# Where a decoder layer's matmul operands begin in SBUF, and a shorter product of P and V

## The chip, the core and the metric

The kernel runs on one core of a Trainium2 chip. Its time is the time of one execution on the device in microseconds (us), as the median of several runs. One further execution is recorded by the hardware profiler; all rows called profile come from it. A core has a matrix engine (TensorE, PE in the profile; PEld is its loading of the stationary operand, the "weights" of a matmul), VectorE (DVE), ScalarE (ACT), GpSimd (POOL) and SyncE (SP, which here issues the transfers). They work on two memories on the chip: SBUF, with 128 partitions, in which all tiles below lie, and PSUM, into which matmuls write. A tile begins at the same byte in each partition it uses, and "remainder" below is that byte modulo 512.

## The reference

One layer of a decoder with 256 positions and 2048 channels, in float32. Cut to what matters:

```python
h = rmsnorm(x, pre_mix_g)
proj = h @ w_in                  # q, k, v of two groups of heads, and forget gates
o_a = swa_sink_attention(...)    # 16 heads, 2 key/value heads, window 128, sinks, ALiBi
o_b = forgetting_attention(...)  # 16 heads, decay from the forget gates
mix = concatenate([rmsnorm(o_a), rmsnorm(o_b)]) @ w_out
x = x + rmsnorm(mix, post_mix_g)
h = rmsnorm(x, pre_ffn_g)
u = causal_dwconv(h @ w_up)      # width 3; 2 x 5632 channels
gate, val = split(u, 2)
x = x + rmsnorm((gelu(gate) * val) @ w_down, post_ffn_g)
```

## The kernel before

**High and low parts.** To keep float32 accuracy with TensorE's fp32r type, each operand a is kept as two tiles: a high part, a rounded to fp32r, and a low part, the rest. A product is three matmuls: high by high, low by high, high by low. The weights come from memory in units of up to 1024 columns (`w_load`, tile `raw`); ACT writes the high part (L104, tile `whi`) and DVE the low part (L107, tile `wlo`), each in one of five rotating buffers. The activations lie as high part in columns 0 to 255 and low part in columns 256 to 511 of one row: `hT` (16 blocks of 128 channels, the normed and transposed input), `oT` (16 tiles, attention's output) and `G` (22 tiles, the gated channels).

**Which operand is held.** A matmul has a held operand of 128 columns, loaded ahead of it, and a moving one that streams past it. In the projections to q and k and to the feed-forward channels (`proj_T`, `unit_T`) the weights are held and hT moves. A high pass (L247) streams 512 columns, both parts of hT, past a block of `whi`; a low pass (L254) streams the 256 high columns past a block of `wlo`. For each pair of output blocks the runs are: 16 matmuls of the high pass for blocks 0 to 7 of hT, 32 of the low pass for all blocks, 16 of the high pass for blocks 8 to 15. In `mm3` (L269) the roles are exchanged: a block of hT (V projection), oT (output projection) or G (down projection) is held, and 512 columns of `whi` or `wlo` move. There, six matmuls in a row belong to one tile: for each half of the positions high by `whi`, high by `wlo`, low by `whi`.

**Where the tiles begin.** Rows of hT, oT and G have 520 elements, of which 512 are used (`WIDE = 520`, 2080 bytes). So block k of hT begins at remainder 32k, and each tile of oT and G begins 32 bytes further on than the one before it in SBUF. `raw`, `whi` and `wlo` have 1024 columns and begin at multiples of 512, except for eight tiles of a later pool that hold parts of the output projection.

**Attention.** Work for a pair of heads is cut into stages (`tables`, `scores`, `transposes`, `pv`), which `later` and `tick` put between the units of the projections, so that TensorE has projections to do while DVE and ACT work on the softmax. In `pv` both parts of V are held: 128 columns for a pair of heads, the same 64 values twice in the first group, where two heads share them. P's parts `ph` and `pl` stream past them, 512 columns (L478) and then 256 (L480). The upper 64 rows of the result are one head's output and the lower 64 the other's, each in its own columns. ACT and DVE take these from PSUM (L487 to L489).

**Order.** TensorE's instructions stand in the order in which the program is written (`manual_schedule`). The other engines are ordered by a scheduler outside a few written stretches.

Of the kernel before, what the change touches and what calls it, by code (L numbers as in the profile page):

```python
# [17 lines left out]
P = 128  # L18
# [4 lines left out]
KT = D // P  # L23
EPS = 1e-6
NEG = -1e30
FHALF = 22
HOLD = 6
WIDE = 520


@with_exitstack
def hybrid_layer(ctx: ExitStack, tc: tile.TileContext, x, pre_mix_g, w_in, b_forget, sinks,
# [3 lines left out]
    pe, act, dve, pool, sp = nc.tensor, nc.scalar, nc.vector, nc.gpsimd, nc.sync  # L36
# [4 lines left out]
    const = ctx.enter_context(tc.tile_pool(name="const", bufs=1))  # L41
    main = ctx.enter_context(tc.tile_pool(name="main", bufs=1))
    wp = ctx.enter_context(tc.tile_pool(name="wp", bufs=4))
    small = ctx.enter_context(tc.tile_pool(name="small", bufs=4))
    ps = ctx.enter_context(tc.tile_pool(name="ps", bufs=1, space=PSUM))

    ctx.enter_context(tc.manual_schedule(engines={mybir.EngineType.PE}))

    def bank(tag="acc"):
# [14 lines left out]
    UNIT = 1024  # L64
    WB = 5

    def w_load(src, a, c, pin=False):
        raw = wp.tile([P, UNIT], F32, tag="raw", bufs=5, name="raw")
        i = sp.dma_start(raw[:, :a * c].rearrange("p (a c) -> p a c", a=a), src)
        if pin:  # L70
            tc.keep_in_program_order(i)
        return raw, a, c

    def w_parts(n, keep=None):

        if keep and keep[0] is None:
            return keep[1]
        where, pre, nb = (keep[0], "h", keep[1]) if keep else (wp, "w", WB)
        return [where.tile([P, UNIT], F32R, tag=pre + x, bufs=nb, name="w" + x)[:, :n]
                for x in ("hi", "lo")]  # L80

    def w_high(unit, keep=None):

        raw, a, c = unit
        n = a * c
        hi, lo = w_parts(n, keep)
        act.copy(hi, raw[:, :n])

        def low():
            dve.tensor_tensor(lo, raw[:, :n], hi.bitcast(F32), op=ALU.subtract)  # L90

        return [x.rearrange("p (a c) -> p a c", a=a) for x in (hi, lo)], low

    def w_split(unit, pin=False, keep=None, begun=None, between=None):

        raw, a, c = unit
        n = a * c
        hi, lo = begun or w_parts(n, keep)
        for i in range(2 if between else 1):
            cs = slice(i * 512, i * 512 + 512) if between else slice(0, n)  # L100
            if i:
                between()
            if not between or i:
                i1 = act.copy(hi[:, cs], raw[:, cs])  # L104
                if pin:
                    tc.keep_in_program_order(i1)
            i2 = dve.tensor_tensor(lo[:, cs], raw[:, cs], hi[:, cs].bitcast(F32), op=ALU.subtract)  # L107
            if pin:
                tc.keep_in_program_order(i2)
        return [x.rearrange("p (a c) -> p a c", a=a) for x in (hi, lo)]  # L110

    def w_unit(src, a, c, keep=None):
        return w_split(w_load(src, a, c), keep=keep)

    def w_rows(w, k0, a, c0, c):
        return w[k0 * P:(k0 + a) * P, c0:c0 + c].rearrange("(a p) c -> p a c", p=P)
# [10 lines left out]
    gpre = const.tile([16, P], F32, tag="gpre", name="gpre")  # L127
# [7 lines left out]
    for i in range(2):  # L135
        cs = slice(i * 256, (i + 1) * 256)
# [26 lines left out]
    gcol = const.tile([P, 48], F32, tag="gcol", name="gcol")  # L163
# [9 lines left out]
        pool.tensor_tensor(r, v, mhalf, op=ALU.pow)  # L173
        return r

    hT = main.tile([P, KT, WIDE], F32R, tag="hT", name="hT")
    def to_T(srcs, t0, n, g0, pin=False):

        for part in range(2):
# [91 lines left out]
    def split(hi, lo, src):  # L271
        act.copy(hi, src)
        dve.tensor_tensor(lo, src, hi.bitcast(F32), op=ALU.subtract)

    with tc.tile_pool(name="mixp", bufs=1) as mp:
        oT = [mp.tile([P, WIDE], F32R, tag="oT", bufs=16, name=f"oT{j}")[:, 0:512] for j in range(16)]
        sqs = mp.tile([P, 2, S], F32, tag="sqs", name="sqs")

        att = tc.tile_pool(name="att", bufs=1)
        ap = att.__enter__()  # L280
# [44 lines left out]
        begun = w_parts(UNIT)  # L325
# [4 lines left out]
        for u in range(4):  # L330
            if u:
                parts = w_split(first[0][u], True)
            else:
                parts = w_split(first[0][u], True, begun=begun,
                                between=lambda: x_part(0, (1,), "acc"))
# [17 lines left out]
            unit_T(parts, u, bq0)  # L353


        gst = const.tile([32, P], F32, tag="gst", name="gst")
        sp.dma_start(gst[0:16, :], pre_ffn_g.rearrange("o (a p) -> (o a) p", p=P))
        sp.dma_start(gst[16:24, :], grp_swa_g.rearrange("o (a p) -> (o a) p", p=P))
        sp.dma_start(gst[24:32, :], grp_fox_g.rearrange("o (a p) -> (o a) p", p=P))
# [24 lines left out]
            pool.affine_select(out=u, in_=u, compare_op=ALU.is_ge, fill=0.0, base=base,  # L384
                               pattern=[[1, 256]], channel_multiplier=-1)

        vpa = ap.tile([P, 2, 2, 2, P], F32R, tag="vpa", name="vpa")
        vpb = main.tile([P, 2, 2, 8, P], F32R, tag="x", name="vpb")

        NK = 3  # L390
# [27 lines left out]
        def attend(j, q, ki, values, table, h0, sink, at):  # L418
# [53 lines left out]
            def pv():  # L472
                ph, pl = st["h"], st["l"]
                o = bank("att")
                ov = o.rearrange("p (e q) -> p e q", e=2)
                passes = ((0, ph), (1, ph), (0, pl))
                for n, (hl, p) in enumerate(passes):
                    pe.matmul(ov, values(hl, 0), p[:, :, 0:256], start=(n == 0), stop=False)  # L478
                for n, (hl, p) in enumerate(passes):
                    pe.matmul(ov[:, :, P:256], values(hl, 1), p[:, :, 256:384], start=False,  # L480
                              stop=(n == 2))
                sq = ap.tile([P, 256], F32, tag="sqo", bufs=1, name="sqo")
                for e in range(2):
                    r = slice(e * 64, (e + 1) * 64)
                    g = gcol[r, 32 + j:33 + j]
                    hi, lo = oT[j][r, 0:256], oT[j][r, 256:512]
                    act.activation(hi, ov[r, e, :], AF.Copy, scale=g)  # L487
                    act.activation(sq[r, :], ov[r, e, :], AF.Square)
                    dve.scalar_tensor_tensor(lo, ov[r, e, :], g, hi.bitcast(F32), op0=ALU.mult,  # L489
                                             op1=ALU.subtract)  # L490
# [13 lines left out]
        def swa_pair(p, q, at):  # L504
            def table(t):
                for e in range(2):
                    slope = 2.0 ** (-8.0 * (2 * p + e + 1) / H)
                    pool.tensor_scalar(t[:, e, 0:256], dist, -slope, None, op0=ALU.mult)
                    pool.tensor_scalar(t[:, e, 256:384], dist[:, P:256], -slope, None,
                                       op0=ALU.mult)  # L510

            attend(p, q, p // 4, lambda hl, t: vpa[:, hl, t, p // 4, :], table, 2 * p, True, at)

        cq = ap.tile([P, 2, H], F32, tag="cq", name="cq")

# [23 lines left out]
        def kv_a():  # L539
            k32 = scratch()  # L540
            evac_sum(bkv[0], k32, rowk)
            ksw = scratch()
            sp.dma_start(ksw[64:128, :], k32[0:64, :])
            sp.dma_start(ksw[0:64, :], k32[64:128, :])
            for i, (e_src, o_src) in enumerate(((k32, ksw), (ksw, k32))):
                for r, src in zip(halves, (e_src, o_src)):
                    split(khi[i][r, :], klo[i][r, :], src[r, :])
            v32 = scratch()
            evac_sum(bkv[1], v32, rowk)

            def v_T():
                vb = bank("att")
                for t in range(2):
                    pe.transpose(vb[:, t * P:(t + 1) * P], v32[:, t * P:(t + 1) * P], ident)
                vv = vb[:, :256].rearrange("p (t k d) -> p t k d", t=2, k=2)
                for e in range(2):
                    split(vpa[:, 0, :, :, e * 64:(e + 1) * 64],
                          vpa[:, 1, :, :, e * 64:(e + 1) * 64], vv)

            later(3, v_T)  # L560

# [121 lines left out]
        out_half(1, evac_b, range(2))  # L683


        hT2 = main.tile([P, KT, WIDE], F32R, tag="hT", name="hT2")
        hT = hT2
        dffn, rmix = [], []
        sq2 = [small.tile([P, 4], F32, tag=f"sqm{t}", bufs=1, name=f"sqm{t}") for t in range(2)]
# [53 lines left out]
        for n in (2, 3):  # L743
            for u in range(4):
                raw = w_load(w_rows(w_out, 8 + u * 2, 2, n * 512, 512), 2, 512)
                (hi, lo), low = w_high(raw, (hp, 4) if n == 2 else None)
# [41 lines left out]
    with tc.tile_pool(name="ffn", bufs=1) as fp:  # L788
# [87 lines left out]
        ysq = [small.tile([P, 5], F32, tag=f"ysq{t}", bufs=1, name=f"ysq{t}") for t in range(2)]  # L876
        gbf = None
        for half in range(2):
            G = [fp.tile([P, WIDE], F32R, tag="G", bufs=FHALF, name=f"G{j}")[:, 0:512]
                 for j in range(FHALF)]  # L880
            for g in range(FHALF // 2):
                c0 = (half * (FHALF // 2) + g) * 256
# [75 lines left out]
        held = []  # L958
# [61 lines left out]
```

## Time and profile before

| | |
|---|---|
| runs | 1096.8, 1095.73, 1096.19 us; median 1096.19 |
| profiled execution | 1095.65 us, its span 1093.9 us |
| TensorE, matmul | 1082.4 us busy (99%), 6002 instructions |
| TensorE, loading of weights | 930.1 us busy (85%) |
| VectorE, ScalarE | 729.3 us (67%), 613.7 us (56%) |
| mean traffic | 185 GB/s; HBM read 199.58 MB |
| granted TensorE clock | 0.998 of full speed |

The span runs from the first to the last instruction; the execution's time holds 1.75 us more. A row of a group gives line, engine, operation and tiles (written <- read), then busy time and the mean duration of one in ns, then the idle time before it. A matmul's duration is longer than the step from its start to the next one's start, since each begins while the one before it drains. So steps are read from starts, or from a run of known length.

### The profile page before, as it was taken

How to read it: one execution, taken by the hardware profiler on the slowest of the kernel's cores; microseconds unless marked ns; L12 is line 12 of the kernel's file. 1: busy time of each engine (PE TensorE's matmuls, PEld its weight loads, DVE VectorE, ACT ScalarE, POOL GpSimd, SP SyncE). 2: the span in 40 equal slices, each digit the busy share in tenths (PEclk: the TensorE clock that was granted, in tenths of full speed). 3: DMA queues.
4: the chain of work that ended last, by engine and by line, in shares of the span. 5: the costliest groups of instructions: out<-in, count | busy, mean ns of one | idle time of the engine just before them, and what ended most of it. 6: DMA issues, size and time to landing. Idle time of an engine off the chain costs nothing.

```text
span 1093.9 us, 16309 instructions
## 1 busy us (share of the span) xinstructions
PE 1082.4 (99%) x6002; PEld 930.1 (85%) x6002; DVE 729.3 (67%) x1193; ACT 613.7 (56%) x1069; POOL 223.5 (20%) x252
## 2 busy tenths in 40 slices
PE   9999999999999999999999999999999999999996
PEld 7899988888889888888888888888888888888886
DVE  5977767776468876777677444457777777755453
ACT  7766766667547655556555443446555555644450
POOL 3342343441022212112121000002121211201111
PEclk9999999999999999999999999999999999999999
DMA  8645557554863766666655665666566656656552
GB/s 290 207 117 168 173 155 220 164 161 151 288 218 117 228 187 184 191 192 191 187 183 182 198 189 188 188 188 192 177 192 189 185 184 192 190 193 187 185 169 78
DMA packets 164971, 202.88 MB, mean 185 GB/s; under 512 B 6780, under 2 KB 130972, under 8 KB 164380
## 3 DMA queue, kind: packets, MB, share of 16 engines
q1 hardware_dynamic: 164176, 201.27, 59.3%
q8 instruction: 47, 0.77, 0.3%
q10 hardware_dynamic: 716, 0.58, 0.2%
q14 instruction: 32, 0.26, 0.1%
HBM read 199.58 MB, written 2.11 MB: 184 GB/s over the span
## 4 chain that ended last, share of the span: by engine, by line
PE 97%; DVE 1%; ACT 1%; DMA 0%; issue 0%; POOL 0%; SPq 0%; DVEq 0%; POOLq 0%; ACTq 0%
PE bank_acc L269 35%; PE bank_acc L247 22%; PE bank_att L247 14%; PE bank_acc L254 12%; PE bank_att L254 7%; PE bank_att L434 1%; PE bank_att L478 1%; PE bank_att L469 1%; PE bank_att L211 1%; PE bank_acc L211 1%; PE bank_att L480 1%; DVE wlo L107 0%; DMA x_in<-in_x_dram 0%; PE bank_att L216 0%; DVE hT L715 0%; PE bank_acc L216 0%
## 5 line engine op out<-in xcount | busy, mean ns | idle before, releaser
L107 DVE TENSOR_TENSOR wlo<-raw,whi 128x1024 fp32r<-128x1024 f32 (+3 forms) x357 | 429.4, 1211 | 265.4 <-ACT whi L104 256.0
L104 ACT CAST whi<-raw 128x1024 fp32r<-128x1024 f32 (+3 forms) x356 | 363.0, 1033 | 291.4 <-issue 140.9
L247 PE MATMUL bank_acc<-hT,whi 128*128 128x512 f32 x1088 | 263.9, 395 | 0.0
L247 PEld LDWEIGHTS bank_acc<-hT,whi 128*128 128x128 f32 x1088 | 200.6, 188 | 43.7
L269 PE MATMUL bank_acc<-whi,G 128*128 128x512 f32 (+1 forms) x724 | 217.8, 383 | 0.0
L824 POOL TENSOR_TENSOR u<-u,rowf 128x256 f32<-128x256 f32 x88 | 96.8, 1121 | 508.2 <-DVE u L823 505.9
L269 PEld LDWEIGHTS bank_acc<-whi,G 128*128 128x128 f32 x724 | 133.6, 188 | 29.4
L247 PE MATMUL bank_att<-hT,whi 128*128 128x512 f32 x640 | 153.6, 394 | 0.0
L247 PEld LDWEIGHTS bank_att<-hT,whi 128*128 128x128 f32 x640 | 118.8, 188 | 26.8
L254 PE MATMUL bank_acc<-hT,wlo 128*128 128x256 f32 x1088 | 139.5, 282 | 0.0
L254 PEld LDWEIGHTS bank_acc<-hT,wlo 128*128 128x128 f32 x1088 | 135.3, 188 | 4.4
L269 PE MATMUL bank_acc<-wlo,G 128*128 128x512 f32 (+1 forms) x362 | 138.9, 384 | 0.0
L269 PE MATMUL bank_acc<-whi,oT 128*128 128x512 f32 (+1 forms) x272 | 83.5, 383 | 0.0
L269 PEld LDWEIGHTS bank_acc<-wlo,G 128*128 128x128 f32 x362 | 68.0, 188 | 14.6
L254 PEld LDWEIGHTS bank_att<-hT,wlo 128*128 128x128 f32 x640 | 78.5, 188 | 1.8
L254 PE MATMUL bank_att<-hT,wlo 128*128 128x256 f32 x640 | 79.1, 281 | 0.0
L269 PEld LDWEIGHTS bank_acc<-whi,oT 128*128 128x128 f32 x272 | 50.1, 188 | 10.3
L269 PE MATMUL bank_acc<-wlo,oT 128*128 128x512 f32 (+1 forms) x136 | 51.8, 381 | 0.0
L269 PE MATMUL bank_acc<-whi,hT 128*128 128x384 f32 (+1 forms) x192 | 47.7, 325 | 0.0
L826 ACT ACTIVATE yg<-u,cw 128x256 f32<-128x256 f32 x44 | 26.5, 602 | 26.7 <-POOL u L824 26.7
L826 ACT ACTIVATE yv<-u,cw 128x256 f32<-128x256 f32 x44 | 26.5, 602 | 25.9 <-POOL u L824 25.9
L452 ACT ACTIVATE p<-p,nm 128x256 f32<-128x256 f32 (+1 forms) x64 | 28.4, 445 | 20.3 <-DVE nm L440 20.3
(195 smaller groups left out, 1012.5 us busy)
## 6 DMA issues: line engine op xcount, KB each, us to landing
raw<-in_w_up_dram SPq DMA_DIRECT2D x176, 512.0 KB, 3.6
raw<-in_w_down_dram SPq DMA_DIRECT2D x88, 512.0 KB, 4.6
raw<-in_w_in_dram SPq DMA_DIRECT2D x51, 512.0 KB, 4.3
raw<-in_w_out_dram SPq DMA_DIRECT2D x32, 512.0 KB, 4.4
raw<-in_w_in_dram SPq DMA_DIRECT2D x16, 384.0 KB, 3.7
cb<-c_dram SPq DMA_DIRECT2D x8, 256.0 KB, 3.4
x_sb<-in_x_dram SPq DMA_DIRECT2D x2, 1024.0 KB
raw<-in_w_in_dram SPq DMA_DIRECT2D x5, 408.0 KB, 3.5
```

The source lines that it names most:

```text
L104: i1 = act.copy(hi[:, cs], raw[:, cs])
L107: i2 = dve.tensor_tensor(lo[:, cs], raw[:, cs], hi[:, cs].bitcast(F32), op=ALU.subtract)
L211: pe.matmul(b, hi[:, a, m * P:(m + 1) * P], hT[:, kt, 0:512], start=(kt == 0), stop=(kt == KT - 1))
L247: pe.matmul(b, hi[:, a, m * P:(m + 1) * P], hT[:, kt, 0:512], start=(kt == 0), stop=(last == (0, kt)))
L254: pe.matmul(b[:, 256:512], lo[:, a, m * P:(m + 1) * P], hT[:, u * 4 + a, 0:256], start=False, stop=(last == (1, u * 4 + a)))
L269: pe.matmul(b, a, r[:, cols], start=(first and i == 0), stop=(last and i == 2))
L434: pe.matmul(sb[e][:, cs], a[r, t * P:(t + 1) * P], b[r, 0:nk], start=(n == 0), stop=(n == 2))
L452: act.activation(p[:, e, cs], p[:, e, cs], AF.Exp, bias=nm[:, t, e:e + 1], scale=-1.0, accum_out=rs[:, t, e:e + 1])
L469: pe.transpose(pb[:, i * P:(i + 1) * P], p[:, e, c:c + P], ident)
L478: pe.matmul(ov, values(hl, 0), p[:, :, 0:256], start=(n == 0), stop=False)
L824: pool.tensor_tensor(u[:, 2:258], u[:, 2:258], rowf, op=ALU.mult)
L826: act.activation(y, u[:, 2:258], AF.Identity, bias=cw[:, 3, ch:ch + 1], scale=cw[:, 2, ch:ch + 1])
```

## The change

**Where operands begin.** The rows of hT, oT and G have 512 elements now. A filler before hT puts all its 16 blocks at remainder 192 (a filler behind it, one in the small pool and the reuse of `gpre`'s tile for `gst` bring what comes after to where it is wanted). All tiles of oT and G, and all tiles of moving weights, begin at multiples of 512. High parts that are held still begin there too. Low parts get buffers of 1152 columns in the common pool: as moving operand they begin at the buffer's start, as held operand 56 elements (224 bytes) behind it (`LOW`, argument `held`).

**The first group's V.** Its tile held 64 high values twice, and 64 low values twice in another block. Now one block holds the 64 high values beside the 64 low ones (`vpa`, half as large), and `pv` makes two passes, `ph` and `pl`, instead of three. The result's upper 64 rows are P by high and its lower 64 rows P by low, for both heads; so ACT copies the lower rows to a tile `half`, DVE adds them to the upper rows into a scratch tile, and the gain, the square and the low part of oT are then made from that for both heads at once. P low by V low is added by this as well, which was left out before.

```diff
+LOW = 56
+ROOM = 112
+    small.tile([P, ROOM], F32, tag="room", bufs=1, name="room")
...
+    def w_parts(n, keep=None, held=True):
...
+        hi = where.tile([P, UNIT], F32R, tag=pre + "hi", bufs=nb, name="whi")
+        if where is not wp:
+            lo = where.tile([P, UNIT], F32R, tag=pre + "lo", bufs=nb, name="wlo")
+            return hi[:, :n], lo[:, :n]
+        lo = where.tile([P, UNIT + 128], F32R, tag=pre + "lo", bufs=nb, name="wlo")
+        return hi[:, :n], lo[:, LOW * held:LOW * held + n]
...
     def w_unit(src, a, c, keep=None):
-        return w_split(w_load(src, a, c), keep=keep)
+        return w_split(w_load(src, a, c), keep=keep, held=False)
...
-    hT = main.tile([P, KT, WIDE], F32R, tag="hT", name="hT")
+    main.tile([P, 48], F32, tag="before_hT", name="before_hT")
+    hT = main.tile([P, KT, 512], F32R, tag="hT", name="hT")
+    main.tile([P, 80], F32, tag="behind_hT", name="behind_hT")
...
-        oT = [mp.tile([P, WIDE], F32R, tag="oT", bufs=16, name=f"oT{j}")[:, 0:512] for j in range(16)]
+        oT = [mp.tile([P, 512], F32R, tag="oT", bufs=16, name=f"oT{j}")[:, 0:512] for j in range(16)]
...
-        gst = const.tile([32, P], F32, tag="gst", name="gst")
+        gst = const.tile([32, P], F32, tag="gpre", name="gst")
...
-        vpa = ap.tile([P, 2, 2, 2, P], F32R, tag="vpa", name="vpa")
+        vpa = ap.tile([P, 2, 2, P], F32R, tag="vpa", name="vpa")
...
-                passes = ((0, ph), (1, ph), (0, pl))
+                passes = ((0, ph), (0, pl)) if sink else ((0, ph), (1, ph), (0, pl))
...
+                if sink:
+                    half = ap.tile([64, 512], F32, tag="half", bufs=1, name="half")
+                    act.copy(half, o[64:128, :])
+                    ob = scratch()
+                    for e in range(2):
+                        cs = slice(e * 256, (e + 1) * 256)
+                        dve.tensor_tensor(ob[e * 64:(e + 1) * 64, :], o[0:64, cs], half[:, cs],
+                                          op=ALU.add)
+                    g = gcol[:, 32 + j:33 + j]
+                    hi, lo = oT[j][:, 0:256], oT[j][:, 256:512]
+                    act.activation(hi, ob, AF.Copy, scale=g)
+                    act.activation(sq, ob, AF.Square)
+                    dve.scalar_tensor_tensor(lo, ob, g, hi.bitcast(F32), op0=ALU.mult,
+                                             op1=ALU.subtract)
...
-                for e in range(2):
-                    split(vpa[:, 0, :, :, e * 64:(e + 1) * 64],
-                          vpa[:, 1, :, :, e * 64:(e + 1) * 64], vv)
+                split(vpa[:, :, :, 0:64], vpa[:, :, :, 64:128], vv)
...
-            G = [fp.tile([P, WIDE], F32R, tag="G", bufs=FHALF, name=f"G{j}")[:, 0:512]
+            G = [fp.tile([P, 512], F32R, tag="G", bufs=FHALF, name=f"G{j}")[:, 0:512]
```

Where operands begin changes no order. P times V does. On TensorE, around the first `pv` of the first group (between low passes of a projection; `vpa` is V, `ph` and `pl` are P's parts), before:

```order
L254 MATMUL bank_acc<-hT,wlo 128x256 x8
L478 MATMUL bank_att<-ph,vpa 128x512 x2
L478 MATMUL bank_att<-pl,vpa 128x512
L480 MATMUL bank_att<-ph,vpa 128x2x128 x2
L480 MATMUL bank_att<-pl,vpa 128x2x128
L254 MATMUL bank_acc<-hT,wlo 128x256 x8
```

And of the change (L487 and L489 are the lines before's L478 and L480, L263 is L254):

```order
L263 MATMUL bank_acc<-hT,wlo 128x256 x8
L487 MATMUL bank_att<-ph,vpa 128x512
L487 MATMUL bank_att<-pl,vpa 128x512
L489 MATMUL bank_att<-ph,vpa 128x2x128
L489 MATMUL bank_att<-pl,vpa 128x2x128
L263 MATMUL bank_acc<-hT,wlo 128x256 x8
```

One matmul of each width has gone, and the place between the low passes is the same. On ACT, which takes the result from PSUM, at the first pair, before:

```order
L452 ACTIVATE p,rs<-p,nm 128x128 x2
L487 ACTIVATE oT_114<-bank_att,gcol 64x256
L488 ACTIVATE sqo<-bank_att 64x256
L449 ACTIVATE es<-es 128x4
L399 COPY scr<-bank_acc 128x256 x2
L487 ACTIVATE oT_114<-bank_att,gcol 64x256
L488 ACTIVATE sqo<-bank_att 64x256
```

And of the change:

```order
L461 ACTIVATE p,rs<-p,nm 128x128 x2
L494 COPY half<-bank_att 64x512
L408 COPY scr<-bank_acc 128x256
L458 ACTIVATE es<-es 128x4
L408 COPY scr<-bank_acc 128x256
L111 CAST whi<-raw 128x768
L502 ACTIVATE oT_117<-scr,gcol 128x256
L503 ACTIVATE sqo<-scr 128x256
```

The four operations of 64 rows have become one copy of 64 rows and two operations of 128 rows; these two stand behind the copy and DVE's two additions.

More of the change, by code (lines that the diff above doesn't have):

```diff
@@ L27 @@
 HOLD = 6
-WIDE = 520
+LOW = 56
+ROOM = 112
 @with_exitstack
@@ L72, in w_load @@
         return raw, a, c
-    def w_parts(n, keep=None):
+    def w_parts(n, keep=None, held=True):
         if keep and keep[0] is None:
@@ L78, in w_parts, with w_high @@
         where, pre, nb = (keep[0], "h", keep[1]) if keep else (wp, "w", WB)
-        return [where.tile([P, UNIT], F32R, tag=pre + x, bufs=nb, name="w" + x)[:, :n]
-                for x in ("hi", "lo")]
-    def w_high(unit, keep=None):
+        hi = where.tile([P, UNIT], F32R, tag=pre + "hi", bufs=nb, name="whi")
[4 more added lines that the diff above has]
+        return hi[:, :n], lo[:, LOW * held:LOW * held + n]
+    def w_high(unit, keep=None, held=True):
         raw, a, c = unit
         n = a * c
-        hi, lo = w_parts(n, keep)
+        hi, lo = w_parts(n, keep, held)
         act.copy(hi, raw[:, :n])
@@ L92, in w_high, with w_split @@
         return [x.rearrange("p (a c) -> p a c", a=a) for x in (hi, lo)], low
-    def w_split(unit, pin=False, keep=None, begun=None, between=None):
+    def w_split(unit, pin=False, keep=None, begun=None, between=None,
+                held=True):
         raw, a, c = unit
         n = a * c
-        hi, lo = begun or w_parts(n, keep)
+        hi, lo = begun or w_parts(n, keep, held)
         for i in range(2 if between else 1):
@@ L480, in pv @@
                     pe.matmul(ov[:, :, P:256], values(hl, 1), p[:, :, 256:384], start=False,
-                              stop=(n == 2))
+                              stop=(n == len(passes) - 1))
                 sq = ap.tile([P, 256], F32, tag="sqo", bufs=1, name="sqo")
-                for e in range(2):
+                if sink:
[12 more added lines that the diff above has]
+                                             op1=ALU.subtract)
+                for e in () if sink else range(2):
                     r = slice(e * 64, (e + 1) * 64)
@@ L510, in table @@
                                        op0=ALU.mult)
-            attend(p, q, p // 4, lambda hl, t: vpa[:, hl, t, p // 4, :], table, 2 * p, True, at)
+            attend(p, q, p // 4, lambda hl, t: vpa[:, t, p // 4, :], table, 2 * p, True, at)
         cq = ap.tile([P, 2, H], F32, tag="cq", name="cq")
@@ L555, in v_T @@
                 vv = vb[:, :256].rearrange("p (t k d) -> p t k d", t=2, k=2)
-                for e in range(2):
-                    split(vpa[:, 0, :, :, e * 64:(e + 1) * 64],
-                          vpa[:, 1, :, :, e * 64:(e + 1) * 64], vv)
+                split(vpa[:, :, :, 0:64], vpa[:, :, :, 64:128], vv)
             later(3, v_T)
@@ L683, in hybrid_layer @@
         out_half(1, evac_b, range(2))
-        hT2 = main.tile([P, KT, WIDE], F32R, tag="hT", name="hT2")
+        hT2 = main.tile([P, KT, 512], F32R, tag="hT", name="hT2")
         hT = hT2
@@ L745, in hybrid_layer @@
                 raw = w_load(w_rows(w_out, 8 + u * 2, 2, n * 512, 512), 2, 512)
-                (hi, lo), low = w_high(raw, (hp, 4) if n == 2 else None)
+                (hi, lo), low = w_high(raw, (hp, 4) if n == 2 else None, False)
                 low()
```

## The prediction

> **What bounds the kernel now.** I read the page first, then the chain in order of time, then rows of TensorE (PE) in ever smaller windows.
>
> ```profile
> PE 1082.4 (99%) x6002; PEld 930.1 (85%) x6002; DVE 729.3 (67%) x1193; ACT 613.7 (56%) x1069; POOL 223.5 (20%) x252
> ...
> PE 97%; DVE 1%; ACT 1%; DMA 0%; issue 0%; POOL 0%; SPq 0%; DVEq 0%; POOLq 0%; ACTq 0%
> ```
>
> PE works 99% of the span and is 97% of the chain. Of all its waits for others the longest is at the start:
>
> ```profile
> PE bank_acc L159 <- DVE junk L154: 1.3, 1, 1.3
> ```
>
> So time can be won only inside the matmul stream: fewer matmuls, or less time from one start to the next. The chain in order of time gives that step for long runs:
>
> ```profile
> 375.41 7.43 PE bank_att L247 x32
> ...
> 592.44 122.82 PE bank_acc L269 x528
> ```
>
> A 512-wide matmul takes 7.43/32 = 232.2 ns in the high passes of `proj_T` (L247, hT moves) and 122.82/528 = 232.6 ns in the down projection (L269, weights move, G is loaded). These are means. The ninth group of six in that block belongs to G8, since 592.44 + 8 x 6 x 0.2326 = 603.6; here are PE's rows from G7 into G8, and the L269 rows of the two windows (durations as minimum/median/maximum, ns):
>
> ```profile
> 602.28 0.40 PE L269 MATMUL bank_acc<-wlo,G 128*128 128x512 f32 x1
> 602.51 0.63 PE L269 MATMUL bank_acc<-whi,G 128*128 128x512 f32 x2
> 602.98 0.40 PE L269 MATMUL bank_acc<-wlo,G 128*128 128x512 f32 x1
> ...
> 603.68 0.39 PE L269 MATMUL bank_acc<-wlo,G 128*128 128x512 f32 x1
> 603.90 0.62 PE L269 MATMUL bank_acc<-whi,G 128*128 128x512 f32 x2
> 604.36 0.39 PE L269 MATMUL bank_acc<-wlo,G 128*128 128x512 f32 x1
> ```
>
> ```profile
> L269 PE MATMUL bank_acc<-wlo,G x2: 395/396/396, 602.3 to 603.0; 128*128 128x512 f32 x2
> ...
> L269 PE MATMUL bank_acc<-wlo,G x2: 389/389/389, 603.7 to 604.4; 128*128 128x512 f32 x2
> ```
>
> Three matmuls take 0.70 us (233 ns each) before G8 and 0.68 us (227 ns) at G8. The shown duration follows: 396 there, 389 here, so step = duration - 162, which I use below. Nothing differs but addresses. In this kernel a G tile is 2080 bytes, so each begins 32 bytes later than its neighbour modulo 512; in the built program G8 (byte 188416) begins at a multiple of 512, as do the moving weights. The weight load of the next matmul reads while this one streams, and how the two addresses stand to each other is worth 6 ns.
>
> The hT rows do the same with the roles exchanged. The kernel sweeps all sixteen remainders and gets their mean; the change fixes one. In one feed-forward stretch:
>
> ```profile
> 382.68 3.96 PE L254 MATMUL bank_att<-hT,wlo 128*128 128x256 f32 x32
> 386.48 3.88 PE L247 MATMUL bank_att<-hT,whi 128*128 128x512 f32 x16
> 390.19 3.89 PE L247 MATMUL bank_acc<-hT,whi 128*128 128x512 f32 x16
> 393.92 3.94 PE L254 MATMUL bank_acc<-hT,wlo 128*128 128x256 f32 x32
> ```
>
> A low pass (L254, 256 wide) takes (386.48 - 382.68)/32 = 118.8 ns a matmul.
>
> **The change part by part.** First the matmuls whose loaded operand is G or oT (L269), 512 wide:
>
> ```profile
> L269 PE MATMUL bank_acc<-whi,G 128*128 128x512 f32 x652 | 206.2, 394 | 0.0
> ...
> L269 PE MATMUL bank_acc<-wlo,G 128*128 128x512 f32 x326 | 128.8, 395 | 0.0
> L269 PE MATMUL bank_acc<-whi,oT 128*128 128x512 f32 x240 | 77.3, 396 | 0.0
> L269 PE MATMUL bank_acc<-wlo,oT 128*128 128x512 f32 x120 | 47.3, 395 | 0.0
> ```
>
> That is 1338. After the change each stands as G8 does now: both operands at multiples of 512. At best all go from 232.6 to 226.7: -7.9 us. The group's mean is a little over that, since the stream reaches the quick step only after its first matmuls; I take 227.6: 1338 x 5.0 ns = **-6.7 us**. At worst oT, broken up by attention, gains nothing and G settles half way: -2.5 us.
>
> Second, the high passes: all of hT at remainder 192, weights at 0. Today only block 6 of hT (6 x 32) stands so. Its two matmuls come in two sorts. One window of each sort, each with the last matmul of block 5 (397 in both), then all of L247 and L254:
>
> ```profile
> L247 PE MATMUL bank_att<-hT,whi x3: 388/392/397, 381.5 to 382.0; 128*128 128x512 f32 x3
> ...
> L247 PE MATMUL bank_acc<-hT,whi x3: 394/397/399, 392.8 to 393.2; 128*128 128x512 f32 x3
> ...
> L247 PE MATMUL bank_acc<-hT,whi x1088: 388/394/504, 32.5 to 961.8; 128*128 128x512 f32 x182
> L247 PE MATMUL bank_att<-hT,whi x640: 388/394/399, 367.7 to 939.4; 128*128 128x512 f32 x160
> ...
> L254 PE MATMUL bank_acc<-hT,wlo x1088: 276/281/387, 36.3 to 958.2; 128*128 128x256 f32 x182
> L254 PE MATMUL bank_att<-hT,wlo x640: 276/281/287, 371.5 to 935.8; 128*128 128x256 f32 x160
> ```
>
> The first pair is 392 and 388 (230 and 226 ns), the second 399 and 394 (237 and 232). The first ends on the quickest step of all (388), the second falls from its first to its second matmul. At G8 the quick step, once reached, held over the three steps shown; so I lean to the quick pair and take 230 ns against 232.2: 1728 x 2.2 = **-3.8 us**. Bounds: 388 throughout is -10.0 us; the second pair's mean of 234.5 is +4.0 us.
>
> Third, the low passes, 1728 of 256 columns: hT at 192, loaded low parts at 224. No row today has a loaded operand off a multiple of 512 in such a pass. By difference, 192 - 224 is -32, as block 15 has today (480 against 0). It too comes in two sorts; each window holds blocks 14 and 15:
>
> ```profile
> L254 PE MATMUL bank_att<-hT,wlo x4: 283/284/287, 386.0 to 386.4; 128*128 128x256 f32 x4
> ...
> L254 PE MATMUL bank_acc<-hT,wlo x4: 279/282/282, 397.2 to 397.6; 128*128 128x256 f32 x4
> ```
>
> They lie on both sides of the median, 281, so I take **0**. Bounds: 276 throughout (-5 ns) is -8.6 us. For the dear end I use block 6, at 192 against 0 today:
>
> ```profile
> L254 PE MATMUL bank_att<-hT,wlo x5: 280/282/287, 383.9 to 384.3; 128*128 128x256 f32 x5
> ```
>
> Its two are 282 and 287, mean 284.5, +3.5 ns: +6.0 us.
>
> Fourth, the first group's P times V: four matmuls in place of six, for eight pairs of heads.
>
> ```profile
> 58.19 0.63 PE L478 MATMUL bank_att<-ph,vpa 128*128 128x512 f32 x2
> 58.66 0.39 PE L478 MATMUL bank_att<-pl,vpa 128*128 128x512 f32 x1
> 58.88 0.40 PE L480 MATMUL bank_att<-ph,vpa 128*128 128x256 f32 x2
> 59.13 0.28 PE L480 MATMUL bank_att<-pl,vpa 128*128 128x256 f32 x1
> ```
>
> One 512-wide goes, (58.66 - 58.19)/2 = 0.235 us, and one 256-wide, (59.13 - 58.88)/2 = 0.125 us: 8 x 0.36 = **-2.9 us**. PE doesn't wait for what follows. Per pair ACT now does:
>
> ```profile
> L487 ACT ACTIVATE oT<-bank_att,gcol 64x256 fp32r<-64x256 f32 x14 | 6.5, 464 | 2.9 <-DVE oT L489 2.9
> L488 ACT ACTIVATE sqo<-bank_att 64x256 f32<-64x256 f32 x14 | 5.1, 365 | 0.0
> L591 ACT ACTIVATE vpb<-bank_acc,rpre 128x384 fp32r<-128x384 f32 x4 | 2.1, 575 | 0.6 <-PE bank_acc L269 0.6
> ...
> L489 DVE SCALAR_TENSOR_TENSOR oT<-bank_att,gcol,oT 64x256 fp32r<-64x256 f32 x14 | 6.7, 481 | 2.4 <-ACT sqo L488 2.2
> ```
>
> That is 2 x (464 + 365) = 1.66 us on ACT and 2 x 0.48 on DVE. After: one copy of 512 columns (about 0.6, an estimate from L591's 575 ns for 384), one activation, one square, 1.4 us; DVE three operations of about 0.48, +0.5 us, or 4 us over the eight pairs. DVE is 67% busy over the span, so this is hidden; with that cover gone it is those 4 us. The new wait is DVE's for the copy `half`, and queued behind it are splits of weights (L107) that PE needs only units later. The DMA of `gst` now shares the first gains' tile, whose one reader runs in the first 5 us. No price.
>
> Fifth, the V projection also loads hT at 192 now, some 300 matmuls: within +-6 ns each, +-1.8 us; I take 0.
>
> Sum: -6.7 - 3.8 + 0 - 2.9 = -13.4 us on the profiled execution's 1095.65 (span 1093.9 and 1.75 around it) gives 1082.2. The median of the runs lies 0.5 above that execution, so **1082.7**, say 1083.
>
> Against all this speaks a rule of the Trainium skill, "SBUF — State Buffer", section "Who interferes with whom": TensorE has separate ports for moving operand and weight load, and never waits on anyone. By it only the fourth part would count. The trace differs: 396 against 389 ns at G7 and G8.
>
> **The rivals.** *Both passes lock*: high at 388, low at 276, L269 at 226.7: -10.0 - 8.6 - 7.9 - 2.9 = -29.4, 1067. For it: the quick step held at G8 once reached, and a constant remainder gives it time. Against it: block 6's second sort, and its low matmuls of 282 and 287.
>
> *Addresses do nothing*, and the quick rows have another reason, such as their place in the unit: then only P times V counts, 1096.2 - 2.9 = 1093.3. For it speaks only the rule just named. Against it: the G7 and G8 rows, in the same places of their groups.
>
> *One remainder settles slow*: sixteen remainders average out, one need not. If the high passes sit at 234.5 (+4.0), the low ones at block 6's mean (+6.0) and L269 gains only its worst bound of 2.5, then 4.0 + 6.0 - 2.5 - 2.9 = +4.6, 1100.8. It decides from where the two passes lose over 5.4 us together. For it: the second sort; against: the pairs fall from 237 to 232, so that sort doesn't look lasting.
>
> **How the numbers follow.** Forecast, 1074 to 1091: 60%. Both lock, below that: 17%. Nearly only P times V, 1091 to 1096: 13%. Settles slow: 10%. The range 1069 to 1094 leaves out about 5% below and 14% above. About 0.2% (2.2 us) is what a measurement of this kernel can tell from no change. Faster by more, below 1094: 0.60 + 0.17 + 0.09 = 0.86. Within it: 0.06; slower: 0.08.
>
> **What would show it.** In the changed profile: L269's 512-wide rows at a mean near 390 in place of 394 to 396, and a down projection of 528 matmuls in about 120.2 us in place of 122.8. The high rows near 392; the low rows near 281; in the row of P times V 8 matmuls of `ph,vpa` of each width in place of 16; idle time of PE unchanged. I am wrong if L269's mean stays at 394, if the low rows move more than 2 ns either way, or if PE begins to wait for `whi`, `wlo` or `oT`.

## The result: 1086.9 us after 1096.1, and the profile after

| | before | after |
|---|---|---|
| runs | 1095.73 to 1096.8, median 1096.07 | 1086.57 to 1087.42, median 1086.9 |
| profiled execution, its span | 1095.65, 1093.9 us | 1086.65, 1084.9 us |

The ratio is 0.9916, with a 95% interval of 0.9899 to 0.9933: 9.2 us less, where 13.4 were forecast. The first part of the page of the kernel after, and the shares of its chain:

```profile
PE 1073.4 (99%) x5986; PEld 926.5 (85%) x5986; DVE 734.1 (68%) x1200; ACT 613.6 (57%) x1060; POOL 224.8 (21%) x252
...
PE 96%; DVE 1%; ACT 1%; DMA 1%; SPq 0%; issue 0%; POOL 0%; DVEq 0%; POOLq 0%; ACTq 0%
```

TensorE (PE) is still the whole of it. Outside its busy time the span holds 1084.9 - 1073.4 = 11.5 us, and before it held 1093.9 - 1082.4 = 11.5. So in sum no waiting came or went; all 9.0 us lie inside the matmul stream. The chain in order of time says in which stage. Its rows give start, length (us) and what ran. First before, then after, where `mm3` is now L278, the high pass L256 and the low pass L263:

```profile
282.92 50.31 PE bank_acc L269 x216
...
371.63 3.78 PE bank_att L254 x32
...
592.44 122.82 PE bank_acc L269 x528
...
722.77 7.44 PE bank_acc L247 x32
...
962.24 123.08 PE bank_acc L269 x594
```

```profile
279.82 49.13 PE bank_acc L278 x216
...
367.34 3.78 PE bank_att L263 x32
371.12 7.46 PE bank_att L256 x32
...
588.28 119.70 PE bank_acc L278 x528
...
715.50 7.47 PE bank_acc L256 x32
...
955.70 120.64 PE bank_acc L278 x594
```

The stages between these rows, in us:

| stage | before | after | difference |
|---|---|---|---|
| start to the long block of the output projection | 282.92 | 279.82 | -3.10 |
| from there to the first whole low pass of the feed-forward part | 88.71 | 87.52 | -1.19 |
| rest of the first half's up projection | 220.81 | 220.94 | +0.13 |
| first half's down projection | 122.82 | 119.70 | -3.12 |
| second half's up projection | 246.98 | 247.72 | +0.74 |
| second half's down projection | 123.08 | 120.64 | -2.44 |
| tail | 8.58 | 8.56 | -0.02 |

The gain is where weights move (output and down projections) and in the attention part. The up projections, the longest stages, lost 0.9 us. The groups say the same by line, operation and shape, with busy time and the mean duration of one (ns):

```profile
L256 PE MATMUL bank_acc<-hT,whi 128*128 128x512 f32 x1088 | 264.9, 395 | 0.0
L278 PE MATMUL bank_acc<-whi,G 128*128 128x512 f32 x652 | 202.7, 389 | 0.0
...
L278 PE MATMUL bank_acc<-wlo,G 128*128 128x512 f32 x326 | 126.9, 389 | 0.0
...
L278 PE MATMUL bank_acc<-whi,oT 128*128 128x512 f32 x240 | 76.2, 392 | 0.0
L278 PE MATMUL bank_acc<-wlo,oT 128*128 128x512 f32 x120 | 46.7, 389 | 0.0
```

G and oT fell from 394 to 396 down to 389 (392 for `whi,oT`). The high passes stand at 395, not at the forecast 392.

### The profile page after: what moved, and what is told of

Its sections match the earlier page's. It is cut to its first block, busy times and chain, and to the rows that moved or that the text cites. A ratio compares the mean times of both kernels' runs of the same rounds, so it can differ in the third digit from the quotient of the medians.

```text
span 1084.9 us, 16263 instructions
## 1 busy us (share of the span) xinstructions
PE 1073.4 (99%) x5986; PEld 926.5 (85%) x5986; DVE 734.1 (68%) x1200; ACT 613.6 (57%) x1060; POOL 224.8 (21%) x252
## 4 chain that ended last, share of the span: by engine, by line
PE 96%; DVE 1%; ACT 1%; DMA 1%; SPq 0%; issue 0%; POOL 0%; DVEq 0%; POOLq 0%; ACTq 0%
PE bank_acc L278 35%; PE bank_acc L256 23%; PE bank_att L256 14%; PE bank_acc L263 12%; PE bank_att L263 7%; PE bank_att L443 1%; PE bank_att L478 1%; PE bank_att L487 1%; PE bank_acc L220 1%; DMA x_in<-in_x_dram 1%; PE bank_att L220 1%; DVE wlo L114 0%; PE bank_att L489 0%; DVE hT L736 0%; PE bank_acc L225 0%; PE bank_acc L878 0%
## 5 line engine op out<-in xcount | busy, mean ns | idle before, releaser
L256 PE MATMUL bank_acc<-hT,whi 128*128 128x512 f32 x1088 | 264.9, 395 | 0.0
L256 PEld LDWEIGHTS bank_acc<-hT,whi 128*128 128x128 f32 x1088 | 200.3, 188 | 45.0
L278 PE MATMUL bank_acc<-whi,G 128*128 128x512 f32 (+1 forms) x724 | 214.4, 378 | 0.0
L278 PEld LDWEIGHTS bank_acc<-whi,G 128*128 128x128 f32 x724 | 133.7, 188 | 25.6
L256 PE MATMUL bank_att<-hT,whi 128*128 128x512 f32 x640 | 154.1, 395 | 0.0
L256 PEld LDWEIGHTS bank_att<-hT,whi 128*128 128x128 f32 x640 | 118.6, 188 | 27.4
L263 PE MATMUL bank_acc<-hT,wlo 128*128 128x256 f32 x1088 | 139.5, 282 | 0.0
L263 PEld LDWEIGHTS bank_acc<-hT,wlo 128*128 128x128 f32 x1088 | 135.6, 188 | 4.3
L278 PE MATMUL bank_acc<-wlo,G 128*128 128x512 f32 (+1 forms) x362 | 137.1, 379 | 0.0
L278 PE MATMUL bank_acc<-whi,oT 128*128 128x512 f32 (+1 forms) x272 | 82.4, 380 | 0.0
L263 PEld LDWEIGHTS bank_att<-hT,wlo 128*128 128x128 f32 x640 | 78.6, 188 | 1.8
L263 PE MATMUL bank_att<-hT,wlo 128*128 128x256 f32 x640 | 79.0, 281 | 0.0
L278 PEld LDWEIGHTS bank_acc<-wlo,G 128*128 128x128 f32 x362 | 68.1, 188 | 12.8
L278 PEld LDWEIGHTS bank_acc<-whi,oT 128*128 128x128 f32 x272 | 50.2, 188 | 9.2
L278 PE MATMUL bank_acc<-wlo,oT 128*128 128x512 f32 (+1 forms) x136 | 51.2, 377 | 0.0
L278 PE MATMUL bank_acc<-whi,hT 128*128 128x384 f32 (+1 forms) x192 | 47.6, 324 | 0.0
```

Of the source, the lines that this page charges most:

```text
L256: pe.matmul(b, hi[:, a, m * P:(m + 1) * P], hT[:, kt, 0:512], start=(kt == 0), stop=(last == (0, kt)))
L263: pe.matmul(b[:, 256:512], lo[:, a, m * P:(m + 1) * P], hT[:, u * 4 + a, 0:256], start=False, stop=(last == (1, u * 4 + a)))
L278: pe.matmul(b, a, r[:, cols], start=(first and i == 0), stop=(last and i == 2))
```

## The experiments

After the result the theory was this. The step of a matmul stream depends on the remainders of its two operands only through their **difference**, moving minus held, and a stream settles after some matmuls on a step that belongs to that difference. The block of 528 after takes 119.70/528 = 226.7 ns a matmul at difference 0; the high passes take 7.46/32 = 233.1 ns at difference 192. Rivals were that the role decides (moving hT can't reach the quick step), that a remainder shared by all tiles is enough, whichever it is, and that addresses do nothing. All kernels are the changed kernel with the edit shown (the last two start from the kernel with hT at 0), and leave out nothing of the reference.

### Sweeping the held high parts

Held high parts get room to begin at 32 x (call number modulo 16) bytes; held low parts begin at multiples of 512.

```diff
+    sweep = [0]
...
+        hi = where.tile([P, UNIT + 128], F32R, tag=pre + "hi", bufs=nb, name="whi")
...
+        at = sweep[0] * held
+        return hi[:, at:at + n], lo[:, :n]
...
+        def swept(w, c, banks):
+            was, sweep[0] = sweep[0], calls[0] % 16 * 8
+            calls[0] += 1
+            proj_T(w, c, banks, LONG)
+            sweep[0] = was
```

> The changed kernel with the held high parts shifted, in the feed-forward projections, by 0, 32, 64 ... 480 bytes from one call of proj_T to the next (43 calls, so each shift two or three times); the held low parts lie at remainder 0 throughout. hT stays at remainder 192. Theory 'settling' (the distance between the moving operand's and the held operand's remainder sets the step at which a stream settles, and the steps are 226.7 or 233.3 ns): some shifts give high passes at about 227 ns, others at about 233; shift 0 gives 233.3 as in the changed kernel. Rival 'role' (passes in which hT moves can't reach the quick step, because the moving row changes after every second matmul and two PSUM banks alternate): every shift gives 232 to 236 ns. Rival 'addresses do nothing': every shift gives the same mean within 0.3 ns.

Measured: 1082.16 us (one run). In the chain L260 is the high pass and L267 the low one. The rows of 16 high matmuls are second halves of passes at a shift of 64, 128, 192, 256 and 448 bytes, and (429.70) a first half at 224; the row of 32 is the second half at 96 and the first at 128.

```profile
381.50 3.73 PE bank_att L260 x16
...
392.60 7.40 PE bank_acc L260 x32
...
403.77 3.73 PE bank_acc L260 x16
...
411.24 3.64 PE bank_att L267 x32
...
422.27 3.77 PE bank_att L267 x32
426.04 3.66 PE bank_att L260 x16
429.70 3.73 PE bank_acc L260 x16
...
448.30 3.72 PE bank_acc L260 x16
...
515.29 3.66 PE bank_att L260 x16
```

Of the rows of 16 only those at 192 and at 448 are quick, that is at difference 0 modulo 256: 3.66/16 = 228.8 ns a matmul, against 3.72 to 3.73 (233) in the others. So moving hT does reach the quick step, and addresses count: the rivals of the role and of no effect fall. The sweep repeats after 256 bytes, not 512. The kernel as a whole is 4.7 us below the change, but little of that is in the high passes: summed from start to start, the matmuls of the low passes (at difference 192 here) take 3.7 us less than in the change, and those of the high passes 0.8 less. Two things fit no theory held so far. The low passes at 411.24 and 422.27 have the same addresses modulo 512, and took 3.64 and 3.77 us. And at 128 the first half of the high pass took about 3.67 (7.40 less 3.73 for the half at 96), the second 3.73.

### Sweeping the held low parts

The same for the held low parts, with the high ones at multiples of 512. The line that places them (the shift itself is made as in the first sweep):

```diff
-        return hi[:, :n], lo[:, LOW * held:LOW * held + n]
+        return hi[:, :n], lo[:, sweep[0] * held:sweep[0] * held + n]
```

> The changed kernel with the held low parts shifted, in the feed-forward projections, by 0, 32, 64 ... 480 bytes from call to call instead of by 224 always; high parts at remainder 0. 'Settling': the low passes' mean step differs by shift, from about 113.3 ns at the best to 120 or more at the worst; shift 224 gives the 118.3 of the changed kernel; shift 0 is worse than 224, near 120. 'Role': 117 to 119 ns at every shift. 'Addresses do nothing': all within 0.3 ns of 118.3.

Measured: 1086.44 us (one run). The chain's low passes (L265), of shifts 32, 96, 224 (the change's own), 256, 288 and, last, 512 (that is 0 again):

```profile
367.99 3.75 PE bank_att L265 x32
...
390.46 3.83 PE bank_acc L265 x32
...
435.45 3.78 PE bank_acc L265 x32
...
446.69 3.63 PE bank_acc L265 x32
...
457.77 3.76 PE bank_att L265 x32
...
536.47 3.63 PE bank_acc L265 x32
```

The period of 256 bytes is there again (32 and 288, 256 and 512), and 96 is the dearest of the eight. But I had expected shift 0 near 120 ns and worse than 224; it is the best of the eight, 3.63/32 = 113.4 ns, against 118.1 at 224. So for 256 columns the best difference is 192, not 0. The trace of before had pointed the other way: its block 6, at difference 192, was the dear example of the low passes.

### G alone, undone and moved

Two kernels: G's rows with 520 elements again, and all G tiles moved to remainder 64.

```diff
-            G = [fp.tile([P, 512], F32R, tag="G", ...
+            G = [fp.tile([P, 520], F32R, tag="G", ...
```

```diff
+            if half == 0:
+                fp.tile([P, 16], F32, tag="gpad", name="gpad")
             G = [fp.tile([P, 512], F32R, tag="G", ...
```

> The changed kernel with G's rows alone back at 520 elements, so that the held operand of the down projection runs through sixteen remainders again. All else as changed. 'Settling': its 978 matmuls of 512 columns go from 226.8 back to about 232.6 ns: +5.7 us, about 1092.6 us. 'Addresses do nothing': 1086.9.

> The changed kernel with all 22 tiles of G at remainder 64 in place of 0: still one remainder for all. 'Difference': moving minus held is -64, that is 192 modulo 256, at which the first sweep (shift 0) settled at 233.2 ns: the 978 matmuls of 512 columns in the down projection go from 226.8 to about 233.3 ns, +6.3 us, about 1093 us. Rival 'one remainder is enough' (the sixteen remainders cost time because they change from tile to tile): they stay at 227 ns, 1086.9 us.

Measured: 1092.77 us with 520 elements (ratio to before 0.9967, 0.9956 to 0.9978), 5.9 us over the change; 1092.79 with G at 64 (one run), also 5.9 over it. The answer for L278 in the same 100 us of the first down projection, durations as minimum/median/maximum: first the change, then G at 64.

```profile
L278 PE MATMUL bank_acc<-whi,G x295: 389/389/389, 599.7 to 699.7; 128*128 128x512 f32 x148
```

```profile
L278 PE MATMUL bank_acc<-whi,G x286: 394/394/394, 600.0 to 699.6; 128*128 128x512 f32 x143
```

The whole block in the chain of G at 64:

```profile
588.50 123.20 PE bank_acc L278 x528
```

Both streams are perfectly even, one at 389 and one at 394. One remainder for all is not enough; it has to stand right to the moving operand's. G at 64 gives the difference -64, which is 192 modulo 256, the same as in the high passes of the change; and it settles on nearly the same step, 123.20/528 = 233.3 ns where those have 233.1, though the roles are exchanged. That is as slow as sixteen remainders (232.6).

### P times V, undone

```diff
-                passes = ((0, ph), (0, pl)) if sink else ((0, ph), (1, ph), (0, pl))
+                passes = ((0, ph), (1, ph), (0, pl))
```

with V's tile and the steps after the product as before.

> The changed kernel with the first group's V and its product with P as they were before (64 high values twice, three passes, results taken by the old operations on ACT and DVE). Prediction's fourth part: +2.9 us, about 1089.8 us. Rival (the new operations on ACT and DVE hold PE up somewhere, so that part of the saving is lost): less than +2 us.

Measured: 1090.76 us, ratio to before 0.9951 (0.9936 to 0.9965), so 3.9 us over the change; its single runs lie 2.5 to 5.4 over the change's median, which holds the forecast 2.9. In its trace the matmuls of the first group's P times V take 2.8 us more than in the change's, from start to start. The chains of before and after show it in the place itself: P times V of one pair lies between a low run of 8 matmuls and the next block.

```profile
71.16 1.14 PE bank_acc L254 x8
74.31 6.31 PE bank_acc L269 x36
```

```profile
70.75 1.14 PE bank_acc L263 x8
73.54 6.24 PE bank_acc L278 x36
```

From row to row 74.31 - 71.16 = 3.15 us became 73.54 - 70.75 = 2.79: 0.36 a pair, 2.9 us if all eight gain as much.

### hT alone, undone

```diff
-LOW = 56
+LOW = 0
...
-    main.tile([P, 48], F32, tag="before_hT", name="before_hT")
-    hT = main.tile([P, KT, 512], F32R, tag="hT", name="hT")
-    main.tile([P, 80], F32, tag="behind_hT", name="behind_hT")
+    hT = main.tile([P, KT, 520], F32R, tag="hT", name="hT")
...
-        hT2 = main.tile([P, KT, 512], F32R, tag="hT", name="hT2")
+        hT2 = main.tile([P, KT, 520], F32R, tag="hT", name="hT2")
```

> The change with its middle part undone: hT's rows are 520 elements long again and sweep the sixteen remainders, and the held low parts begin at multiples of 512; G, oT and the first group's P times V stay as changed. By the prediction's sum the high passes go back from 230 to 232.2 ns, +3.8 us, 1090.7. By the trace of the changed kernel (high passes at 233.3 ns, low ones at 118.3) they go from 233.3 to 232.2, -1.9 us, and the low passes from 118.3 to 118.8, +0.9 us: 1085.9, about what the change has. If the sum of the high and low parts is really a gain that the rows hide, it is over 1089.

Measured: 1086.21 us, ratio to before 0.9908 (0.9895 to 0.9922). By the prediction's sum it had to be 1090.7. The chain of this kernel (L254 high, L261 low):

```profile
371.52 7.43 PE bank_att L254 x32
378.95 3.80 PE bank_att L261 x32
```

The high rows are back at 7.43. So the part of the change that moved hT and the held low parts brought nothing: without it the time is the same or a little lower (0.7 us, the runs overlapping between 1086.57 and 1086.87).

### Difference 0 for the high passes, 192 for the low ones

hT goes to remainder 0, where the held high parts are. The held low parts go to 64, so that the difference is -64, or 192 modulo 256.

```diff
-LOW = 56
+LOW = 16
...
-    main.tile([P, 48], F32, tag="before_hT", name="before_hT")
-    main.tile([P, 80], F32, tag="behind_hT", name="behind_hT")
+    main.tile([P, 128], F32, tag="behind_hT", name="behind_hT")
```

> The changed kernel with hT at remainder 0 in place of 192, held high parts at 0, held low parts 64 bytes beyond a multiple of 512 in place of 224. So the difference (moving minus held, modulo 256) is 0 in the high passes, as in the first sweep at shift 192, and 192 in the low passes, as in the second sweep at shift 0. Theory 'only the difference counts': high passes 227 to 228.6 ns in place of 233.2 (1728 of them, -8 us), low passes 113.5 or 117.8 ns in place of 118.3 by the state in which they are entered (-8 us or -1 us), V projection a little quicker: about 1078 us, or 1070 us if the low passes take their quick state. Rival 'hT's own remainder counts too': high passes stay at 231 to 234 ns, about 1086 us.

Measured: 1077.79 us, ratio to before 0.9831 (0.9814 to 0.9847), 9.1 us below the change. Chain, and below it the answers for the two lines (L255 high, L262 low) inside one pass each:

```profile
410.11 3.77 PE bank_att L262 x32
413.88 7.28 PE bank_att L255 x32
```

```profile
L255 PE MATMUL bank_att<-hT,whi x30: 388/389/395, 414.2 to 420.8; 128*128 128x512 f32 x30
```

```profile
L262 PE MATMUL bank_att<-hT,wlo x25: 281/281/282, 410.8 to 413.6; 128*128 128x256 f32 x25
```

High: 7.28/32 = 227.5 ns, near the 228.8 at difference 0 with another pair of addresses (192 and 192 in the first sweep). Low: even at 281, 117.8 ns a matmul, though the second sweep had 113.4 at this difference. So the difference sets which steps a stream can settle on, and for the low passes something else chooses between two of them.

### What chooses: the way into the low pass

The candidate is the state in which the run begins. This kernel is the last one, with only the first quarter of each low pass (8 of 32 matmuls, unit 0's held low part) shifted by a further 32 x call bytes. The other 24 have the same addresses, modulo 512, in every call.

```diff
+                shift[0] = first_shift[0] if u == 0 else LOW
                 parts[u] = w_split(...)
+                shift[0] = LOW
...
+            first_shift[0] = (LOW + calls[0] * 8) % 128
```

> The kernel of the run with hT at 0, with only the first quarter of each low pass (8 of 32 matmuls) held at another place, shifted by a further 0, 32, ... 480 bytes from call to call of proj_T in the feed-forward part. 'Entry state': the other 24 low matmuls stand at the same remainders in every call, yet settle at 113.3 ns after some first quarters and at 117.8 after others. Rival 'addresses alone': the 24 have the same mean in every call.

Measured: 1074.12 us (one run). The chain's low passes (L266) for a further shift of 32, 96, 160 and 192, and later 448 (192 again):

```profile
365.88 3.67 PE bank_att L266 x32
...
387.81 3.70 PE bank_acc L266 x32
...
409.74 3.65 PE bank_att L266 x32
...
420.67 3.78 PE bank_att L266 x32
...
508.52 3.78 PE bank_att L266 x32
```

What these rows hold shows inside two of them, at 192 and then at 160, each without its first matmuls:

```profile
L266 PE MATMUL bank_att<-hT,wlo x21: 281/281/283, 421.8 to 424.2; 128*128 128x256 f32 x21
```

```profile
L266 PE MATMUL bank_att<-hT,wlo x22: 276/276/277, 410.7 to 413.1; 128*128 128x256 f32 x22
```

Same kernel, same line and same addresses modulo 512, and yet 276 or 281 by what the eight matmuls before were. Each stays for as long as the run lasts. That addresses alone fix the step falls.

### Both together

The first quarter of every low pass at 224 bytes (the further shift of 160), the rest at 64.

```diff
+    FIRST = 56
...
+                shift[0] = FIRST if u == 0 else LOW
                 parts[u] = w_split(...)
+                shift[0] = LOW
```

> The kernel with hT at remainder 0, held high parts at 0 and held low parts at 64 bytes, but the first quarter of each low pass (unit 0's held low part, 8 of 32 matmuls) at 224 bytes in every call. Nothing else of the two passes differs. Theory (the state in which a run of low matmuls begins decides its step, and moving less held by 32 leads into the quick one): in the 44 long calls the first 8 low matmuls cost about 116.4 ns and the other 24 settle at 113.3 in place of 117.8, the high passes stay at 226.7 settled: 44 x (8 x 1.4 + 24 x 4.4) = 5.1 us off 1077.8, 1072.7 us; the 10 calls that take the low parts in two runs gain at most half as much. Rival (the quick stretches of the kernel with a changing shift came from the change between one call and the next, not from the entry): the 24 stay at 117.8 ns and the time at 1077.8 us.

Measured: **1072.86 us** (1072.57 to 1073.47), ratio to before 0.9787 (0.9773 to 0.9800); the expectation had 1072.7. Chain, and the answer for the low line (L267):

```profile
410.73 3.65 PE bank_att L267 x32
414.39 7.29 PE bank_att L260 x32
```

```profile
L267 PE MATMUL bank_att<-hT,wlo x640: 276/276/282, 366.8 to 916.7; 128*128 128x256 f32 x160
```

The median duration of a low matmul is 276 in place of 281. Here all calls are alike, so the quick step doesn't need a change from one call to the next. This kernel differs from the change only in where operands begin, and beats it by 14.0 us.

## Why the prediction was right and wrong

The sign, the place and the mechanism (steps that hang on how the two operands stand to each other) were right, and 1086.9 lies inside the range. The likeliest time, 1083, was 4 us too low, and one term made more than all of it. By the terms of the prediction, in us. Measured is the time from each matmul's start to the next one's start, waits included, summed over the term's matmuls in both traces, after less before:

| term | forecast | measured |
|---|---|---|
| G and oT, 1338 matmuls of 512 columns | -6.7 | -7.4 |
| high passes, 1728 | -3.8 | +1.5 |
| low passes, 1728 | 0 | 0.0 |
| first group's P times V | -2.9 | -2.8 |
| V projection | 0 | -0.3 |
| the rest | 0 | 0.0 |
| sum | -13.4 | -9.0 |

**G and oT.** Right, by the reason given, and 5.5 ns each where 5.0 was taken. G8 was a fair sample of what all tiles would do: the first down projection runs at 226.7 ns, where 227.6 was taken, and the long block of oT went from 50.31/216 = 232.9 ns to 49.13/216 = 227.5. No run undoes oT alone; its part is read from the rows. G moved to 64 bytes shows that the difference, and not evenness, is what pays.

**The high passes: the step that failed.** The prediction saw block 6 (difference 192) come once as 230 and 226 ns and once as 237 and 232, and took the quick pair to be a stream that reaches a lasting step, because the quick step at G8 had lasted. But G8 stood at difference 0. What belongs to 192 shows after, inside one run of 32 high matmuls, in the answers for L256 at its first five and at 25 later ones:

```profile
L256 PE MATMUL bank_att<-hT,whi x5: 388/393/398, 415.9 to 416.8; 128*128 128x512 f32 x5
```

```profile
L256 PE MATMUL bank_att<-hT,whi x25: 393/393/398, 417.3 to 422.9; 128*128 128x512 f32 x25
```

A 388 is in the entry and in none of the 25 later ones; these go between 393 and 398, 233.2 ns from start to start in the mean. Two matmuls are too few to tell the way into a step from the step. A lasting quick step had been seen at difference 0 only, and the change gave the high passes another one. With difference 0 they do reach it, as the kernel with hT at 0 shows: 7.28 us for 32 in place of 7.43 before, 4.7 ns each and 8.1 us for 1728, most of the cheap bound. (That bound was given as -10.0; with the prediction's own 226 ns for a shown 388 it is 1728 x 6.2 = -10.7.)

**The low passes.** The 0 was right, but partly by luck: it was read from windows of four matmuls at the end of a run, and difference -32 has a lasting step of its own, 118.1 ns, which happens to lie near the 118.8 that the sixteen remainders gave. The bound of block 6 (+3.5 ns at difference 192) had the wrong sign: 192 is the difference with the quickest step, if the run is entered rightly.

**P times V, and the work behind it.** Right in size. The steps that ACT and DVE got in its place stayed hidden, as said: TensorE's idle time is unchanged. One of them cost more than assumed, in the groups of the kernel after, and it made no difference:

```profile
L504 DVE SCALAR_TENSOR_TENSOR oT<-scr,gcol,oT 128x256 fp32r<-128x256 f32 x8 | 6.1, 762 | 0.0
```

The low part of oT took 762 ns on DVE, where 480 were assumed.

**The rivals.** *Both passes lock* (1067) didn't happen with these remainders, but its mechanism exists: with 0, 64 and 224 bytes the same program took 1072.86. *Addresses do nothing* (1093.3) falls: every kernel here but that with the old P times V differs from the change by addresses alone, and they span 1072.86 to 1092.79. The rule of the Trainium skill named there ("SBUF — State Buffer", "Who interferes with whom") says that TensorE waits for no one. Read as the prediction reads it, it leaves nothing for addresses, and the runs differ by 5.9 us for G alone. *One remainder settles slow* was the right picture for the high passes, at 233.1 and not 234.5 ns; the low passes and G did not go that way.

**Still open.** Why the period is 256 bytes, and why the best difference is 0 for 512 columns and 192 for 256. The weight load that runs beside the stream is the candidate, but no run separates it from the moving operand's own reads. That the difference alone counts was tested with a second pair of addresses only at 0 and 192; the other values were seen settled with one pair each.

## What to carry to other kernels

When TensorE is 99% busy, take the step from start to start of each long run of matmuls, and compare runs by the difference between the moving and the held operand's start modulo 256 bytes; here the right differences in 3066 matmuls of 512 columns and 1728 of 256 were worth about 20 us of 1096 (1096.1 less 1072.9, less 2.9 for P times V), with no other instruction saved. Sweep a remainder by call within one kernel, so that one profile shows all of them, and use whole passes: the first matmuls of a stream show how it was entered, not where it settles. A mean over sixteen remainders is a safe middle, and fixing one can lose, as the high passes did.

## What the runs showed of the hardware

- The step of an fp32r matmul stream depends on moving minus held operand's start, with a period of 256 bytes in both sweeps: for 512 columns 226.7 ns at difference 0 and 233.3 at 192; for 256 columns 113.4 to 119.7 ns over the eight differences of the second sweep.
- One pair of addresses can have two lasting steps. At difference 192 the low passes ran at 281 ns or at 276 throughout, by the eight matmuls before them.
- The granted clock was 0.997 to 0.998 in all of these runs, so the differences aren't the clock's.
